# The order of the fill work in the middle stage of a two-layer diffusion block

## The chip, the cores and the metric

The kernel runs on one core of one Trainium2 chip, in fp32 (each matrix product as three matmuls on split operands, see below). The metric is the time of one execution on the device in microseconds, taken as the median of several runs.

## The reference

Two layers work on 256 tokens `x` and 256 context tokens `ctx`, each of width 1024. A layer is a SwiGLU feed-forward, a middle stage of three branches, and a second feed-forward; each has a norm with shift, scale and gate from a modulation vector. The change touches the middle stage only. Cut to that, for the tokens:

```python
zx = modulate(rms_norm(x, norm_g[l, 1]), mx[3], mx[4]) @ w_in[l]
qa, ka, va, qb, kb, vb, ux, gx = split_combined(zx)
qb, kb = apply_axial_rope(qb, cos, sin), apply_axial_rope(kb, cos, sin)
ya = neighborhood_attention(qa, ka, va, ka_c, va_c, na_rpb[l], rows)     # 6 heads
yb = window_attention(qb, kb, vb, kb_c, vb_c, sw_sink[l])                # 6 heads, 2 key heads
yc = conformer_conv(ux, conv_dw_w[l], conv_dw_b[l], conv_ln_g[l], conv_ln_b[l])
ga, gb, gc = jnp.split(jax.nn.sigmoid(gx + b_gate[l]), 3, axis=-1)
x = x + mx[5] * ((ga * (ya @ w_oa) + gb * (yb @ w_ob) + gc * (yc @ w_oc)) @ w_o)
```

`conformer_conv` is a gated linear unit, a depthwise convolution of 31 taps over 256 channels, a layer norm over the channels and a SiLU. The context tokens go through the same in layer 0; in the last layer (layer 1) only their keys and values are needed.

## The kernel before

All activations lie transposed, features on the 128 partitions and tokens along the free axis: 512 columns where both token sets are wanted (layer 0), 256 for `x` alone (layer 1). A product of fp32 accuracy is three matmuls (`mm3`, L316 to L320) on a high and a low part of both operands; the parts are made by `split` (L123): ACT copies the high part, DVE subtracts it for the low one. Weights stream in blocks of 512 KB; each half block is split the same way into `wh` and `wl`, a few blocks ahead of their use. One *step* of a product is one weight tile of 128 x 128, three matmuls.

The middle stage (`middle`, L679) first makes the keys and the gated input of the convolution, the values V and two queries. Then comes a loop (L1118 on) over the attention units `us`. A unit is a pair of heads and an index u: `kind` 0 is the neighbourhood branch, `kind` 1 the window branch, three pairs each; u runs over two halves of the queries of `x` and, in layer 0, a third unit for the context. In round n the program writes:

- `qk`: the scores of unit n into PSUM (`sc`, L987); for the window branch they need the rotated key `kb` and query `qb`;
- `turn`: for the unit before, when a pair's two halves are there, the transposes of the normalised weights `pf` (`pt`, L1048), copied and split by ACT and DVE;
- `soft`: the softmax of unit n on DVE and ACT (L1003 or L1009, exponentials L1020, scaling L1032);
- some steps of the *fill*;
- `pv`: the product with V for the unit before (L1067), and at a pair's end its output `y` (L1075, L1076 and a split).

The fill is a chain of generators (L1088) that is walked a step at a time: the third query of the neighbourhood branch (`query(2)`), gates (`gate(b, f)`, eight steps each, a tanh on ACT at L913; b is the branch, 0 neighbourhood, 1 window, 2 convolution; f one of eight blocks of 128 features), the window branch's key and queries (`key_b`, `query_b`, eight steps each, with a rotation `rope` at L874 that goes through ACT, DVE, POOL, ACT and DVE), and the merges (`merge(b, f)`, L916), that is the output projection of a branch (two steps for the convolution, three for the neighbourhood; `mo`), its product with the gate on DVE (L931) and the sum over branches `M` on POOL (L936). The window branch's merges follow after the loop. The fill is spread evenly: after round n, `nfill * (n + 1) // (N + LA)` of its 208 steps should be done. Steps are taken ahead of that when scores need a query or key that the fill hasn't made yet (the `while` in the loop). Merges of the neighbourhood branch are held back (`before_a`) until its three pairs are done.

Which gates come early is set by `EARLY` (7 in layer 0, 16 in layer 1), over an order of branches 2, 0, 1. So in layer 0 seven gates of the convolution branch come ahead of the window branch's key and queries, in layer 1 all eight of the convolution and all eight of the neighbourhood.

The convolution's taps run on DVE (L791), one for every second fill step. Behind the last tap three parts of its layer norm are put off by a counter of program points (`after`, L758, counted by `tick`, twice as far in the last layer): `mean` 10 points later (mean by a matmul, `cmean` L804, subtraction, squares on ACT, L808), `sums` 8 points after that (sums of squares, L339, square root on ACT, L343, reciprocal and diagonal on DVE, L353), and `rest` 8 points on (the rstd spread over partitions by a matmul, L358, then scale, bias on POOL and SiLU; `yc` is ready at L834, L835). If the first merge of the convolution branch finds no `yc`, it writes out all that is left at once:

```python
        if b == 2 and not ys:
            run(cv, 1 << 20)
            flush()
```

The order in which instructions are written is the order in which each engine takes them, but for a few places where the scheduler interleaves two groups.

Of the kernel before, what the change touches and what calls it, by code (L numbers as in the profile page):

```python
# [19 lines left out]
KD = 8  # L20
# [60 lines left out]
N_POOL = 2  # L81
CV_V = (1, 1)
CV_PACE = (2, 2)
EARLY = (7, 16)
N_FIRST = {0: 3, 1: 7, 2: 5}


# [1 line left out]
def dit_block_kernel(ctx, tc, xT, vec, ident_d, const, crow, gfin, rpb, ws, ada0, adaT, out):  # L89
# [17 lines left out]
    def S(dt=F32, name="s"):  # L107
        return slots.tile([P, 2 * NQ], dt, tag="s", name=nm(name))
# [11 lines left out]
    def f32(ap):  # L120
        return ap.bitcast(F32)
# [12 lines left out]
    for k in range(KD):  # L134
# [19 lines left out]
        out=cs[:, :, 0:2], in_=vt[:, V_C:V_C + 2 * KD].rearrange("p (k s) -> p k s", s=2), func=AF.Silu  # L154
# [524 lines left out]
    def middle(l, norm, nxt):  # L679
        last = l == DEPTH - 1  # L680
# [30 lines left out]
        for parts in fb[:3]:  # L711
            kh, kl = S2("ka")
            for t, sl, b in parts:
                nc.scalar.activation(out=kh[:, sl], in_=t, func=AF.Identity, bias=b)
                nc.vector.scalar_tensor_tensor(
                    out=kl[:, sl], in0=t, scalar=b, in1=f32(kh[:, sl]), op0=ALU.add, op1=ALU.subtract)
            ka.append((kh, kl))
        sg = S(name="sg")
        for s, (pg, pu) in enumerate(zip(fb[3][:nst], fb[4])):
            t, sl, b = pg  # L720
# [4 lines left out]
                out=sg[:, sl], in0=sg[:, sl], scalar1=1.0, scalar2=1.0, op0=ALU.mult, op1=ALU.add)  # L725
            t, sl, b = pu
            nc.vector.scalar_tensor_tensor(
                out=hp[:, 0, s, CPAD:CPAD + NX], in0=t, scalar=b, in1=sg[:, sl], op0=ALU.add, op1=ALU.mult)
# [8 lines left out]
        def now(gen):  # L737
# [12 lines left out]
            out=hp[:, 1, :nst, CPAD:CPAD + NX],  # L750
# [7 lines left out]
        def after(n, fn):  # L758
            due.append([n * (2 if last else 1), fn])
# [13 lines left out]
        def conv():  # L773
            accs = [S(name="cacc") for _ in range(2)]
            cw = small.tile([P, 2 * CONV_W], F32, tag="cw", name=nm("cw"), bufs=1)
            o = V_CW + l * 2 * CONV_W
            nc.vector.tensor_scalar(
                out=cw, in0=vt[:, o:o + 2 * CONV_W], scalar1=0.5, scalar2=None, op0=ALU.mult)
            def wide(t):
                return t[:, qs].rearrange("p (s t) -> p s t", t=NX)  # L780

            for j in range(CONV_W):
                for c in range(2):
                    acc, o = accs[c], c * CONV_W + j
                    x, w = hp[:, c, :nst, j:j + NX], cw[:, o:o + 1]
                    if j == 0:
                        ob = V_CB + l * 2 + c
                        nc.vector.tensor_scalar(
                            out=wide(acc), in0=x, scalar1=w, scalar2=vt[:, ob:ob + 1], op0=ALU.mult, op1=ALU.add)
                    else:  # L790
                        nc.vector.scalar_tensor_tensor(  # L791
                            out=wide(acc), in0=x, scalar=w, in1=wide(acc), op0=ALU.mult, op1=ALU.add)
                    yield
            taps = ring(N_TAP, F32, "ctap")
            sq, res = [], []
            gen = []

            def new(name):
                return next(taps)

            def mean():
                pm = PS("cmean")
                for c in range(2):
                    nc.tensor.matmul(pm[:, qs], onesC, accs[c][:, qs], start=c == 0, stop=c == 1)  # L804
                for c in range(2):
                    nc.vector.tensor_tensor(out=accs[c][:, qs], in0=accs[c][:, qs], in1=pm[:, qs], op=ALU.subtract)
                    q = new("csq")
                    nc.scalar.activation(out=q[:, qs], in_=accs[c][:, qs], func=AF.Square)  # L808
                    sq.append(q)
                after(8, sums)  # L810

            def sums():
                gen.append(inv_rms(sq, qs.stop, onesC[:, 0:1], res, new))
                next(gen[0])
                after(8, rest)

            def rest():
                next(gen[0], None)
                for c in range(2):
                    t = accs[c]  # L820
                    og, ob = V_LG + l * 2 + c, V_LB + l * 2 + c
                    nc.vector.scalar_tensor_tensor(
                        out=t[:, qs], in0=t[:, qs], scalar=vt[:, og:og + 1], in1=res[0][:, qs],
                        op0=ALU.mult, op1=ALU.mult,
                    )
                    nc.gpsimd.tensor_scalar(
                        out=t[:, qs], in0=t[:, qs], scalar1=1.0, scalar2=vt[:, ob:ob + 1], op0=ALU.mult, op1=ALU.add)

                    g = new("cg")
                    nc.scalar.activation(out=g[:, qs], in_=t[:, qs], func=AF.Tanh, scale=0.5)  # L830
                    nc.vector.scalar_tensor_tensor(
                        out=t[:, qs], in0=g[:, qs], scalar=1.0, in1=t[:, qs], op0=ALU.add, op1=ALU.mult)
                    h, lo = pair("yc")
                    nc.scalar.activation(out=h[:, qs], in_=t[:, qs], func=AF.Copy, scale=0.5)  # L834
                    nc.vector.scalar_tensor_tensor(  # L835
                        out=lo[:, qs], in0=t[:, qs], scalar=0.5, in1=f32(h[:, qs]), op0=ALU.mult, op1=ALU.subtract)
                    yc.append((h, lo))

            after(10, mean)

        cv = conv()
# [23 lines left out]
        def query(j):  # L865
            ps = yield from block(QA + j * P, qs)
            qh, ql = pair("q")
            nc.scalar.activation(out=qh[:, qs], in_=ps[:, qs], func=AF.Copy, scale=-QSCALE)
            nc.vector.scalar_tensor_tensor(
                out=ql[:, qs], in0=ps[:, qs], scalar=-QSCALE, in1=f32(qh[:, qs]),  # L870
                op0=ALU.mult, op1=ALU.subtract)
            qa.append((qh, ql))
# [13 lines left out]
        def key_b():  # L886
            ps = yield from block(KB, full)
            z = rope(ps, 1.0, full)
            kh, kl = S2("kb")
            split(kh[:, full], kl[:, full], z[:, full])  # L890
            kb.append((kh, kl))

        def query_b(j):
            ps = PS("qb")
            yield from steps(ps, [W.one("w_in_qb", l, k * P, j) for k in range(KD)], H, qs)
            z = rope(ps, -QSCALE, qs)
            qh, ql = pair("qx")
            split(qh[:, qs], ql[:, qs], z[:, qs])
            qb.append((qh, ql))
# [4 lines left out]
        def gate(b, f):  # L904
            pg = yield from block(GT + b * D + f * P, qs)
            if last and f % 2:
                g = gates[b, f - 1, 0][:, hc]
            else:
                gates[b, f, 0] = S(name="gate")
                g = gates[b, f, 0][:, qs]  # L910
            o = b * KD + f

            nc.scalar.activation(out=g, in_=pg[:, qs], func=AF.Tanh, bias=hb[:, o:o + 1], scale=0.5)  # L913
            gates[b, f] = g

        def merge(b, f):  # L916

            if (b, f) not in gates:
                yield from gate(b, f)
            g = gates.pop((b, f))  # L920
            ys = (ya, yb, yc)[b]
# [3 lines that stand above are left out]
            if b == 1:  # L925
                wts = [W.one("w_out_b_perm", l, j, f * P) for j in range(3)]
            else:
                wts = W.col("w_out_a" if b == 0 else "w_out_c", l, f * P, len(ys))
            ps = PS("mo")
            yield from steps(ps, wts, ys, qs)  # L930
            nc.vector.scalar_tensor_tensor(  # L931
                out=g, in0=g, scalar=1.0, in1=ps[:, qs], op0=ALU.add, op1=ALU.mult)
            if M[f] is None:
                M[f] = g
            elif b != 1:
                nc.gpsimd.tensor_tensor(out=M[f], in0=M[f], in1=g, op=ALU.add)  # L936
            else:
                nc.vector.tensor_tensor(out=g, in0=M[f], in1=g, op=ALU.add)
                h, lo = pair("m")
                split(h[:, qs], lo[:, qs], g)  # L940
                M[f] = (h, lo)
# [141 lines left out]
        def chain(*gens):  # L1083
            for g in gens:
                yield from g

        early = [(b, f) for b in (2, 0, 1) for f in range(KD)][:EARLY[l]]
        fill = chain(  # L1088
            query(2), *(gate(b, f) for b, f in early),
            key_b(), query_b(0), query_b(1), query_b(2),  # L1090
            *(merge(2, f) for f in range(KD)), *(merge(0, f) for f in range(KD)),
        )
        n_early = 5 * KD + len(early) * KD
        before_a = n_early + sum(2 + KD * ((2, f) not in early) for f in range(KD))
        nfill = before_a + sum(3 + KD * ((0, f) not in early) for f in range(KD))
        done = 0

        def step(n):
# [60 lines left out]
    for l in range(DEPTH):  # L1159
        last = l == DEPTH - 1  # L1160
# [137 lines left out]
```

## Time and profile before

| | us |
|---|---|
| median of 3 runs | 2006.89 (2006.39 to 2008.82) |
| the profiled execution, its own time | 2006.36 |
| its span, first to last instruction | 2004.6 |
| PE busy in the span | 1952.5 |
| middle stage's fill loop, layer 0 | about 484 to 705 |
| middle stage's fill loop, layer 1 | about 1618 to 1754 |

A row of the timeline gives the start from the span's beginning, the length and the instruction, output before `<-`, inputs behind it; `x16` is the number of instructions in the row, and a bracket is the idle time of the engine ahead of it with what ended it. Matmuls overlap, so what one costs is read from the start of one to the start of the next. Instructions with two passes (plain fp32 operands) count twice. Engine names: PE is TensorE, DVE VectorE, ACT ScalarE, POOL GpSimd.

### The profile page before, as it was taken

How to read it: one execution, taken by the hardware profiler on the slowest of the kernel's cores; microseconds unless marked ns; L12 is line 12 of the kernel's file. 1: busy time of each engine (PE TensorE's matmuls, PEld its weight loads, DVE VectorE, ACT ScalarE, POOL GpSimd, SP SyncE). 2: the span in 40 equal slices, each digit the busy share in tenths (PEclk: the TensorE clock that was granted, in tenths of full speed). 3: DMA queues.
4: the chain of work that ended last, by engine and by line, in shares of the span. 5: the costliest groups of instructions: out<-in, count | busy, mean ns of one | idle time of the engine just before them, and what ended most of it. 6: DMA issues, size and time to landing. Idle time of an engine off the chain costs nothing.

```text
span 2004.6 us, 29351 instructions
## 1 busy us (share of the span) xinstructions
PE 1952.5 (97%) x10722; PEld 1651.6 (82%) x10722; DVE 1411.7 (70%) x3188; ACT 914.7 (46%) x1763; POOL 105.3 (5%) x100
## 2 busy tenths in 40 slices
PE   7999999999969999999999999999999998899998
PEld 3788888897858888988888888888888988799998
DVE  5887777579656645876667659766674887877654
ACT  4533333354656744533333335333333567767553
POOL 0000000100010101100000010000001001200001
PEclk9999999999979999999999999999999999899999
DMA  7565555423212232354445524554453344255553
GB/s 289 169 202 187 162 175 179 139 90 106 73 41 68 86 99 90 109 177 160 149 157 166 180 90 165 169 156 159 158 168 121 104 140 137 69 184 181 189 185 111
DMA packets 82513, 287.40 MB, mean 143 GB/s; under 512 B 9152, under 2 KB 10944, under 8 KB 81984
## 3 DMA queue, kind: packets, MB, share of 16 engines
q1 hardware_dynamic: 79488, 277.91, 42.2%
q0 software_dynamic: 864, 4.98, 0.7%
q10 hardware_dynamic: 2016, 2.64, 0.4%
q8 instruction: 84, 1.38, 0.3%
q14 instruction: 61, 0.50, 0.1%
HBM read 284.44 MB, written 1.05 MB: 142 GB/s over the span
## 4 chain that ended last, share of the span: by engine, by line
PE 92%; DVE 3%; ACT 2%; DMA 1%; issue 1%; POOL 1%; ACTq 0%; DVEq 0%; POOLq 0%
PE g L319 13%; PE g L320 13%; PE g L318 13%; PE pr L319 8%; PE pr L320 8%; PE pr L318 8%; PE b L318 4%; PE b L319 4%; PE b L320 4%; PE f L318 3%; PE f L319 2%; PE f L320 2%; PE pt L1048 1%; PE sc L987 1%; PE pv L1067 1%; PE mo L318 1%
## 5 line engine op out<-in xcount | busy, mean ns | idle before, releaser
L124 ACT ACTIVATE wh<-raw 128x512 fp32r<-128x512 f32 x760 | 473.6, 631 | 749.4 <-PE g L319 266.4
L125 DVE TENSOR_TENSOR wl<-raw,wh 128x512 fp32r<-128x512 f32 x760 | 524.7, 696 | 187.8 <-PE pr L320 80.9
L245 DVE CUSTOM_DVE_ANT_0 junk<-araw,phase 128x512 f32<-128x512 f32 x512 | 354.8, 693 | 166.6 <-DMA araw<-in_adaT_dram 156.9
L319 PE MATMUL g<-Hl,wh 128*128 128x512 f32 (+1 forms) x1248 | 458.9, 368 | 1.7 <-DVE Hl L479 1.7
L320 PE MATMUL g<-Hh,wl 128*128 128x512 f32 (+1 forms) x1248 | 458.6, 368 | 0.0
L318 PE MATMUL g<-Hh,wh 128*128 128x512 f32 (+1 forms) x1248 | 456.8, 367 | 0.0
L319 PEld LDWEIGHTS g<-Hl,wh 128*128 128x128 f32 x1248 | 234.4, 188 | 44.6 <-DVE Hl L479 2.2
L318 PEld LDWEIGHTS g<-Hh,wh 128*128 128x128 f32 x1248 | 234.6, 188 | 42.7
L320 PEld LDWEIGHTS g<-Hh,wl 128*128 128x128 f32 x1248 | 234.7, 188 | 41.9
L318 PE MATMUL pr<-gh,wh 128*128 128x512 f32 (+1 forms) x704 | 257.6, 366 | 0.0
L320 PE MATMUL pr<-gh,wl 128*128 128x512 f32 (+1 forms) x704 | 257.4, 366 | 0.0
L319 PE MATMUL pr<-gl,wh 128*128 128x512 f32 (+1 forms) x704 | 257.2, 365 | 0.0
L318 PE MATMUL b<-Hh,wh 128*128 128x512 f32 (+1 forms) x480 | 164.8, 343 | 0.8 <-DVE pt L125 0.7
L320 PE MATMUL b<-Hh,wl 128*128 128x512 f32 (+1 forms) x480 | 162.9, 339 | 0.0
L319 PE MATMUL b<-Hl,wh 128*128 128x512 f32 (+1 forms) x480 | 162.8, 339 | 0.0
L319 PEld LDWEIGHTS pr<-gl,wh 128*128 128x128 f32 x704 | 132.2, 188 | 23.4
L318 PEld LDWEIGHTS pr<-gh,wh 128*128 128x128 f32 x704 | 132.3, 188 | 23.2
L320 PEld LDWEIGHTS pr<-gh,wl 128*128 128x128 f32 x704 | 132.2, 188 | 23.1
L318 PE MATMUL f<-qh,wh 128*128 128x258 f32 (+1 forms) x400 | 120.1, 300 | 0.4 <-ACT qh L505 0.4
L319 PE MATMUL f<-ql,wh 128*128 128x258 f32 (+1 forms) x400 | 115.8, 290 | 0.0
L320 PE MATMUL f<-qh,wl 128*128 128x258 f32 (+1 forms) x400 | 115.7, 289 | 0.0
L386 POOL TENSOR_TENSOR sq<-sq,sq 128x512 f32<-128x512 f32 (+1 forms) x36 | 44.1, 1226 | 1278.9 <-ACT sq L379 1276.9
(247 smaller groups left out, 2613.0 us busy)
## 6 DMA issues: line engine op xcount, KB each, us to landing
raw<-in_ws_dram SPq DMA_DIRECT2D x380, 512.0 KB, 3.5
araw<-in_adaT_dram SPq DMA_DIRECT2D x128, 512.0 KB, 4.1
araw<-in_ada_dram SPq DMA_DIRECT2D x32, 256.0 KB, 5.9
phase<-in_crow_dram POOLq DMA_DIRECT2D x3, 1024.0 KB, 6.7
tb<-in_rpb_dram ACTq DMA_DIRECT2D x12, 192.0 KB, 3.8
R<-in_xT_dram SPq DMA_DIRECT2D x8, 256.0 KB, 4.9
phase<-in_const_dram POOLq DMA_DIRECT2D x2, 640.0 KB, 6.3
out_dram<-fin SPq DMA_DIRECT2D x4, 256.0 KB, 2.5
```

Of the source, the lines that this page charges most:

```text
L124: nc.scalar.activation(out=hi, in_=src, func=AF.Copy)
L125: nc.vector.tensor_tensor(out=lo, in0=src, in1=f32(hi), op=ALU.subtract)
L245: nc.vector.tensor_tensor_reduce(out=junk, in0=raw[:, c], in1=self.rows[:, s, c], scale=1.0, scalar=0.0, op0=ALU.mult, op1=ALU.add, accum_ ...
L318: nc.tensor.matmul(ps, wh, xh, start=start, stop=False)
L319: nc.tensor.matmul(ps, wh, xl, start=False, stop=False)
L320: nc.tensor.matmul(ps, wl, xh, start=False, stop=stop)
L386: eng.tensor_tensor(out=a[:, full], in0=a[:, full], in1=sq[:, full], op=ALU.add)
L987: nc.tensor.matmul(pss[s][:, o], a[r, c], b[r, k], start=i == 0, stop=i == 2)
L1048: nc.tensor.transpose(pt[:, n * P:(n + 1) * P], self.pf[v][s][:, o + i * P:o + (i + 1) * P], ident)
L1067: nc.tensor.matmul(self.po[s][:, sl], V[t0 + i][j // 2][:, c:c + P], p[:, k], start=m == 0, stop=m == n - 1)
```

## The change

The chain of the fill is written in another order, and the norm's parts stand 14 points apart in place of 8. Neighbourhood merges now come ahead of convolution merges in both layers, so the early gates are those of the neighbourhood branch first. In layer 0 the seven early gates are replaced by those of branch 0, and the eighth of branch 0 and the first of branch 2 follow the queries. In layer 1 the sixteen early gates stay, but in groups between the key and queries of the window branch: six, key and first query, four, second query, three, third query, three. The number of fill steps stays 208; those ahead of the neighbourhood merges (`before_a`) go from 120 to 112 in layer 0 and from 184 to 168 in layer 1. One line less above it moves the code below by one line, and the new chain moves the last part by six.

```diff
-EARLY = (7, 16)
...
-                after(8, sums)
+                after(14, sums)
...
-                after(8, rest)
+                after(14, rest)
...
-        early = [(b, f) for b in (2, 0, 1) for f in range(KD)][:EARLY[l]]
-        fill = chain(
-            query(2), *(gate(b, f) for b, f in early),
-            key_b(), query_b(0), query_b(1), query_b(2),
-            *(merge(2, f) for f in range(KD)), *(merge(0, f) for f in range(KD)),
-        )
-        n_early = 5 * KD + len(early) * KD
-        before_a = n_early + sum(2 + KD * ((2, f) not in early) for f in range(KD))
-        nfill = before_a + sum(3 + KD * ((0, f) not in early) for f in range(KD))
+        ahead = {b: [(b, f) for f in range(KD)] for b in range(3)}
+
+        def some(b, n):
+            out, ahead[b][:n] = ahead[b][:n], []
+            return [gate(*bf) for bf in out]
+
+        if last:
+            parts = [query(2), *some(0, 6), key_b(), query_b(0), *some(0, 2), *some(2, 2), query_b(1),
+                     *some(2, 3), query_b(2), *some(2, 3)]
+        else:
+            parts = [query(2), *some(0, 7), key_b(), query_b(0), query_b(1), query_b(2), *some(0, 1), *some(2, 1)]
+        before_a = KD * len(parts)
+        nfill = before_a + sum((3 if b == 0 else 2) + KD * ((b, f) in ahead[b]) for b in (0, 2) for f in range(KD))
+        fill = chain(*parts, *(merge(b, f) for b in (0, 2) for f in range(KD)))
```

## The prediction

> **What bounds the kernel now.** The page first, its part on busy time: one engine is busy for nearly all of the span.
>
> ```profile
> PE 1952.5 (97%) x10722; PEld 1651.6 (82%) x10722; DVE 1411.7 (70%) x3188; ACT 914.7 (46%) x1763; POOL 105.3 (5%) x100
> ```
>
> The kernel is bound by TensorE, so the change can only win time in which PE idles or runs slowly. Second, PE's waits (what it waited for: us in total, times, longest).
>
> ```profile
> PE ada L201 <- DMA araw<-in_ada_dram: 12.6, 2, 11.8
> PE sc L987 <- ACT qx L124: 10.8, 3, 5.3
> PE sums L339 <- ACT ctap L808: 9.2, 1, 9.2
> PE mo L318 <- ACT ych L834: 4.8, 1, 4.8
> PE rstd L358 <- DVE ctap L353: 1.6, 1, 1.6
> ```
>
> The first is the kernel's start, which the change doesn't touch. The other four are all in the middle stages: the scores wait for the rotated query (qx), and the convolution's norm (sums, rstd) and its merge (mo) wait for each other. Third, the windows of the stretches in which they fall and of their neighbours (stretch, then its length, busy time of PE, PEld, DVE, ACT, POOL, the granted clock, DMA share, GB/s).
>
> ```profile
> 572.92:602.88 29.96, 14.40 (x59) 9.97 (x58) 14.50 (x29) 11.92 (x21) 5.13 (x6) 0.66 0.05 18
> 1612.37:1660.45 48.08, 47.31 (x384) 44.01 (x382) 40.58 (x106) 37.68 (x84) 0.00 (x0) 1.00 0.40 133
> 1660.45:1694.71 34.26, 34.26 (x261) 32.61 (x260) 21.93 (x44) 24.68 (x50) 3.75 (x4) 1.00 0.53 168
> 1694.71:1732.46 37.75, 26.96 (x142) 21.58 (x141) 31.35 (x77) 26.71 (x63) 5.23 (x6) 0.77 0.12 42
> 1732.46:1745.00 12.54, 12.54 (x107) 11.99 (x105) 11.74 (x33) 11.89 (x29) 2.91 (x3) 1.00 0.37 108
> ```
>
> The clock is part of the loss: 0.66 and 0.77 in the two stretches with waits, 1.00 in the others.
>
> **What goes in layer 0.** Before, PE reaches the first merge of the convolution branch (step 96 of the fill) when its norm has hardly begun, so `flush()` issues all of it on the spot:
>
> ```order
> L320 MATMUL qb_5139<-Hh_3722,wl_5035 128x512
> L804 MATMUL cmean_5190<-cacc_3986,onesC 128x512
> L339 MATMUL sums_5197<-onesC,ctap_5170 128x1
> L358 MATMUL rstd_5213<-ctap_5172,ones 128x512
> L318 MATMUL mo_5236<-ych_5220,wh_5040 128x512
> L1067 MATMUL pv_5243<-pt_4144,v_4117 128x256
> ```
>
> Now (lines one lower) gates (b), attention (pv, sc, pt) and the merges of the neighbourhood branch (mo from y) stand between:
>
> ```order
> L317 MATMUL qb_5139<-Hh_3722,wh_5034 128x512
> L317 MATMUL b_5190<-Hh_3639,wh_5040 128x512
> L803 MATMUL cmean_5267<-cacc_3986,onesC 128x512
> L1066 MATMUL pv_5207<-pt_4144,v_4121 128x256
> L986 MATMUL sc_5330<-kbh_4943,qxh_5029 128x512
> L338 MATMUL sums_5358<-onesC,ctap_5170 128x1
> L317 MATMUL mo_5383<-yh_4655,wh_5197 128x512
> L317 MATMUL mo_5383<-yh_5322,wh_5197 128x512
> L357 MATMUL rstd_5495<-ctap_5172,ones 128x512
> ```
>
> No matmul is added or taken away. What the old stretch cost is read from PE's timeline (start, length, what; a wait in brackets):
>
> ```profile
> 572.92 1.88 PE L804 MATMUL cmean<-cacc,onesC 128*128 128x512 f32 x4
> 583.99 3.67 PE L339 MATMUL sums<-onesC,ctap 128*128 128x1 f32 x16 [9.18 <-ACT ctap L808]
> 589.22 2.05 PE L358 MATMUL rstd<-ctap,ones 128*128 128x512 f32 x2 [1.57 <-DVE ctap L353]
> 596.08 0.80 PE L318 MATMUL mo<-ych,wh 128*128 128x512 f32 x1 [4.81 <-ACT ych L834]
> ...
> 599.11 2.10 PE L1067 MATMUL pv<-pt,v 128*128 128x256 f32 x16
> ...
> 602.88 0.48 PE L318 MATMUL mo<-ych,wh 128*128 128x512 f32 x1
> 603.20 0.39 PE L319 MATMUL mo<-ycl,wh 128*128 128x512 f32 x1
> 603.43 0.40 PE L320 MATMUL mo<-ych,wl 128*128 128x512 f32 x1
> ...
> 1679.68 0.95 PE L339 MATMUL sums<-onesC,ctap 128*128 128x1 f32 x8
> ```
>
> At full clock its content is: mean 1.88; sums 2 x 0.95 = 1.90 (layer 1 has half as many, at clock 1.00); rstd about 0.9 (2.05 at half clock); six merge matmuls at a spacing of 0.23 (603.20 to 603.43), 1.4; from pv to the next merge 602.88 - 599.11 = 3.77, left as it is. Sum 9.85 of 29.96: **20.1 us go**, 15.6 of them the three waits, the rest half-clock matmuls.
>
> What is late next there: between mean and sums now lie 33 matmuls of 0.23, a half pv (1.0) and scores (0.9), 9.5 us, against 9.2 that PE waited before; between sums and rstd, and rstd and the first convolution merge, over 11 us each, against 1.6 and 4.8. The third head pair's y is needed 6.3 us after its pv (scores 0.9, nine matmuls 2.1, sums 1.9, six merge matmuls 1.4). An earlier pair's y took 3.6 us, from copy to residue:
>
> ```profile
> 556.38 1.22 ACT L1075 ACTIVATE yf<-pv 64x512 f32<-64x512 f32 x2
> 559.33 0.69 DVE L125 TENSOR_TENSOR yl<-yf,yh 128x512 fp32r<-128x512 f32 x1
> ```
>
> The new wait lies between 0 and about 5 (the old wait for ych, were y as late); I take 0.5, since both covers exceed the rows that they have to hide.
>
> **What goes in layer 1.** Before, all sixteen gates came ahead of the key and the queries of the window branch. Its first scores need them, so at step 96 the program runs 56 fill steps in one lump, and the six window scores then have almost no fill between them:
>
> ```order
> L987 MATMUL sc_15118<-kbh_15038,qx_15101 128x512
> L1048 MATMUL pt_15126<-ident,pf_13949 128x128
> L1067 MATMUL pv_15168<-pt_13953,v_13926 128x256
> L987 MATMUL sc_15193<-kbh_15038,qx_15101 128x512
> L318 MATMUL qb_15246<-Hh_13452,wh_15049 128x256
> L987 MATMUL sc_15260<-kbh_15038,qx_15243 128x512
> ```
>
> Now a gate, a query and the mean stand between transposes and pv, and two gates behind the scores:
>
> ```order
> L986 MATMUL sc_14813<-kbh_14594,qx_14644 128x512
> L1047 MATMUL pt_14821<-ident,pf_13949 128x128
> L317 MATMUL b_14865<-Hh_13452,wh_14740 128x256
> L317 MATMUL qb_14901<-Hh_13452,wh_14780 128x256
> L803 MATMUL cmean_14933<-cacc_13795,onesC 128x256
> L1066 MATMUL pv_14943<-pt_13953,v_13926 128x256
> L986 MATMUL sc_14968<-kbh_14594,qx_14644 128x512
> L317 MATMUL b_15000<-Hh_13452,wh_14872 128x256
> ```
>
> The old stretch on PE, from the second query's end at 1694.71, and below it the same groups at full clock:
>
> ```profile
> 1700.21 0.79 PE L987 MATMUL sc<-kbh,qx 64*128 64x512 f32 x2 [5.34 <-ACT qx L124]
> ...
> 1701.79 3.57 PE L1048 MATMUL pt<-ident,pf 128*128 128x128 f32 x16
> ...
> 1714.50 0.50 PE L987 MATMUL sc<-kbh,qx 64*128 64x512 f32 x2 [1.93 <-ACT qx L124]
> ...
> 1715.41 3.59 PE L1048 MATMUL pt<-ident,pf 128*128 128x128 f32 x16
> ...
> 1727.59 0.80 PE L987 MATMUL sc<-kbh,qx 64*128 64x512 f32 x2 [3.52 <-ACT qx L124]
> ...
> 1732.46 0.36 PE L318 MATMUL mo<-yc,wh 128*128 128x256 f32 x1
> ```
>
> ```profile
> 1632.59 1.97 PE L1048 MATMUL pt<-ident,pf 128*128 128x128 f32 x16
> 1634.31 0.37 PE L318 MATMUL b<-Hh,wh 128*128 128x256 f32 x1
> ...
> 1734.67 2.04 PE L1067 MATMUL pv<-pt,v 128*128 128x256 f32 x16
> 1736.64 0.50 PE L987 MATMUL sc<-kbh,qx 64*128 64x512 f32 x2
> ...
> 1737.54 0.39 PE L318 MATMUL mo<-yc,wh 128*128 128x256 f32 x1
> 1737.77 0.28 PE L319 MATMUL mo<-yc,wh 128*128 128x256 f32 x1
> 1737.88 0.28 PE L320 MATMUL mo<-yc,wl 128*128 128x256 f32 x1
> ```
>
> Content: five scores of 0.90 (1736.64 to 1737.54), three times sixteen transposes of 1.72, two pv of 1.97, a query block of 24 matmuls at about 0.118 with 0.12 at its start, 2.95, and six merge matmuls, 0.83: 17.4 of 37.75. **20.4 us go**, 10.8 of them waits.
>
> What is late next: ACT and DVE. From 1660.45 to 1745.00 (three rows of the windows) PE needs 84.55 - 20.4 = 64.2 us; ACT was busy for 24.68 + 26.71 + 11.89 = 63.3 us in it, DVE for 65.0. The key's rotation moves ahead of that stretch, two steps on ACT like the one below and these on DVE:
>
> ```profile
> 1692.61 0.64 ACT L124 ACTIVATE kbh<-rot 128x512 fp32r<-128x512 f32 x1 [1.44 <-POOL rot L883]
> 1689.73 1.74 DVE L880 SCALAR_TENSOR_TENSOR rot<-b,phase 32x256 f32<-32x256 f32 x4 [0.17 <-ACT rot L877]
> 1693.39 0.88 DVE L125 TENSOR_TENSOR kbl<-rot,kbh 128x512 fp32r<-128x512 f32 x1
> ```
>
> That leaves ACT 63.3 - 1.2 = 62.1 and DVE 65.0 - 2.6 = 62.4, both 97% of PE's time. The row 1732.46:1745.00 has 95% and 94% with PE never waiting, so new waits can be 0. The longest stretch that ran well, 1612.37:1660.45, holds 78% of ACT and 84% of DVE; if 85% of ACT were the most that lasts, the same work would take 62.1 / 0.85 = 73.1 us, PE would wait 8.9, and three slow groups of transposes (3.57 against 1.97) would add 4.8: 13.7. I take 4.5, nearer to the first: the mix is the same, but the norm's table loads and the queries' rotations now stand in ACT's queue between the exponentials, which wait behind them, and the next transposes with these.
>
> Those loads are there before too, one row of them:
>
> ```profile
> 1680.47 1.28 ACT L343 ACT_TABLE_LOAD   x1
> 1681.77 0.26 ACT L343 ACTIVATE sd<-sums,eps 128x2 f32<-128x2 f32 x1
> ```
>
> They now lie between a pair's exponentials and its scaling, on which the next transposes wait. By this row the two switches hold ACT for 2.6 us, which the 63.3 contain. [...]
>
> **Edits at nothing.** Convolution taps keep their steps, weights the distance at which they are loaded (DMA share at most 0.53 above). POOL's adds move from the one branch to the other; in layer 1 eight follow within 16 steps, and the last branch's merges, eleven steps each, hide them; uncovered they'd cost the few us by which they trail.
>
> **The sum.** Against the profiled execution (2006.36, span 2004.6 and 1.8 around it; the median of the runs is 0.5 above): 20.1 + 20.4 - 0.5 - 4.5 = 35.5, so 1970.9; against the median, **1971.4**. No new wait at all gives 1966.4, both upper bounds, 5 and 13.7, give 1985.1; the forecast's own range is 1966 to 1977.
>
> **Rivals.** *ACT sets the pace* in layer 1: 13.7 in place of 4.5, 1980.6; for it the 97%, against it the row 1732.46:1745.00. Chance 0.18, for 1977 to 1982.
>
> *The rotated queries stay late.* The first scores came 8.4 us after their query's block (1694.71 - 2.95 to 1700.21). Now 72 matmuls of 0.118, a pv and a score lie between, 11.4 us; but the key's rotation precedes it on a busier ACT, which then stands waiting on POOL with the copies of y and the exponentials behind. All three late gives back 20.4 less the 4.5: 1987.3. Chance 0.08.
>
> *Slower: the clock stays down.* Place: layer 1's window loop, transposes behind scores. After a wait of only 1.93 the transposes at 1715.41 took 3.59, half clock. If a short gap in each round keeps PE there, 64.2 us of content take up to twice that; once two thirds of it do (40.5 saved of 60 lost) the kernel is slower, at worst 2026. Against it: 1.00 in 1612.37:1660.45, with 0.8 us idle. Chance 0.03. [...]
>
> *Nothing comes of it*: the lost time turns up elsewhere in the stage; the order above speaks against it. Chance 0.03, within 0.2% (about what a measurement of this kernel can tell from no change).
>
> **The numbers.** Forecast 0.68, rivals 0.18, 0.08, 0.03, 0.03. Faster 0.68 + 0.18 + 0.08 = 0.94, same 0.03, slower 0.03. The range goes from just under no new waits, 1965.5, to the end of the first rival, 1982.
>
> **What would show it.** Right: PE's waits for ctap, ych and qx gone or under 1 us each, clock 1.00 through layer 0's middle, the layer 1 window loop near 69 us from the same scores to the same transposes; what waits are left, transposes on pf or scores on qx. Wrong: waits of several us on pf, pt or y, or a clock below 0.9 in that loop.

## The result and the profile after

The changed kernel takes 1976.78 us (median of 4 runs, 1976.24 to 1977.84) against 2006.64 us before (2006.35 to 2008.82): a ratio of 0.985, 95% interval 0.9832 to 0.9867. That is 29.9 us less, where 35.5 were forecast; the time lies in the forecast's own range (1966 to 1977), 0.2 us inside its end. The first rival begins there, so the time alone doesn't tell the two apart. The profiled execution of the changed kernel took 1976.25 us, its span is 1974.5.

The page's line on busy time shows the same instructions in a shorter span: PE's busy time fell by 10.9 us, the rest of the 30.1 us between the spans was idle time.

```profile
PE 1941.6 (98%) x10722; PEld 1644.0 (83%) x10722; DVE 1406.1 (71%) x3188; ACT 909.7 (46%) x1763; POOL 103.5 (5%) x100
```

PE's waits after (us in total, times, longest). The rows for ctap and ych are gone, those for qx went from 10.8 to 0.7; small new ones stand in their place. Lines are one lower than before.

```profile
PE ada L200 <- DMA araw<-in_ada_dram: 13.3, 2, 12.2
PE pt L1047 <- ACT pf L1031: 3.6, 5, 1.1
PE b L317 <- DVE pt L124: 2.2, 2, 1.4
PE cmean L803 <- DVE rot L879: 1.7, 1, 1.7
...
PE sc L986 <- DVE qx L124: 0.4, 1, 0.4
...
PE sc L986 <- ACT qx L123: 0.3, 1, 0.3
```

Where the time came from is read by cutting both traces at the same instructions: the first V product of layer 0, the first of layer 1, and the first product with `w_o` (`pr`) of layer 1. The windows between them (stretch, length, busy time of PE, PEld, DVE, ACT, POOL, clock, DMA share, GB/s), first of before:

```profile
450.44:1590.06 1139.62, 1123.46 (x5406) 923.95 (x5404) 780.93 (x1758) 488.65 (x934) 55.96 (x47) 0.99 0.39 128
1590.06:1783.80 193.74, 182.19 (x1313) 167.01 (x1311) 159.78 (x368) 130.90 (x279) 18.78 (x20) 0.96 0.40 129
```

and of after:

```profile
451.85:1572.14 1120.29, 1117.77 (x5405) 921.28 (x5404) 779.55 (x1758) 486.49 (x934) 56.48 (x47) 1.00 0.40 130
1572.14:1752.77 180.63, 174.54 (x1312) 160.44 (x1311) 155.75 (x368) 128.24 (x279) 16.93 (x20) 1.00 0.42 138
```

Length less PE's busy time is PE's idle time. Layer 0 gained 19.3 us: idle time fell from 16.2 to 2.5 (13.6), busy time by 5.7, for the same matmuls. Layer 1 gained 13.1: idle time from 11.6 to 6.1 (5.5), busy time by 7.6. The start, up to the first V product, took 1.4 us longer (451.85 against 450.44), and what follows layer 1's `pr` 0.9 (1974.5 - 1752.77 = 221.7 against 2004.6 - 1783.80 = 220.8); the change touches neither, and in the twelve traces of the experiments the first V product starts anywhere from 451.1 to 453.0 and the last part takes 220.8 to 222.1, whatever the edit. The 450.44 of before lies 0.7 below that, so not all of the 1.4 is shown to be spread. 19.3 + 13.1 - 1.4 - 0.9 = 30.1.

In layer 0 the chain that PE had waited for now runs behind other work (PE's timeline of after: start, length, instruction, wait in brackets). Sums, root's spread and the merges of y come without a wait, at full clock (1.00 from 572 to 612); a wait that the prediction does not have stands ahead of the mean.

```profile
582.84 1.96 PE L803 MATMUL cmean<-cacc,onesC 128*128 128x512 f32 x4 [1.73 <-DVE rot L879]
...
594.33 1.84 PE L338 MATMUL sums<-onesC,ctap 128*128 128x1 f32 x16
...
596.81 0.39 PE L317 MATMUL mo<-yh,wh 128*128 128x512 f32 x1
...
607.26 1.02 PE L357 MATMUL rstd<-ctap,ones 128*128 128x512 f32 x2
```

The mean comes soon after the third window query's block, and `rot`, which the query's rotation writes, is no input of it; what it must wait for is a buffer that the rotation still reads, a PSUM bank by the code (an inference; the trace names only the rotation).

In layer 1 the largest new waits of the window loop stand at two groups of transposes, behind the first window scores. (Ahead of that loop two gate blocks wait 1.40 and 0.79 us for DVE's split of transposes, the 2.2 of the list above; before had one such wait of 0.7, and in the experiments the first of the two is anything from 0.3 to 1.9.)

```profile
1655.62 1.09 PE L1047 MATMUL pt<-ident,pf 128*128 128x128 f32 x8 [1.04 <-ACT pf L1031]
1657.78 0.99 PE L1047 MATMUL pt<-ident,pf 128*128 128x128 f32 x7 [1.06 <-ACT pf L1031]
```

ACT's timeline shows what made `pf` late: ACT stands for 2.10 us until POOL has finished the rotation of the first query, and a gate, weight copies and the softmax (exponentials L1019, scaling L1031) queue behind that copy.

```profile
1648.87 0.78 ACT L1074 ACTIVATE yf<-pv 64x256 f32<-64x256 f32 x2
1651.76 0.42 ACT L123 ACTIVATE qx<-rot 128x256 fp32r<-128x256 f32 x1 [2.10 <-POOL rot L882]
...
1653.49 0.69 ACT L1019 ACTIVATE pf<-sc,st 128x512 f32<-128x512 f32 x1
...
1654.85 0.72 ACT L1031 ACTIVATE pf<-pf,st 128x512 f32<-128x512 f32 x1
1655.47 0.67 ACT L1019 ACTIVATE pf<-sc,st 128x512 f32<-128x512 f32 x1
...
1657.01 0.71 ACT L1031 ACTIVATE pf<-pf,st 128x512 f32<-128x512 f32 x1
```

### The profile page after: what moved, and what is told of

Read it like the earlier page. It is cut to its first block, busy times and chain, and to the rows that moved or that the text cites. A ratio compares the mean times of both kernels' runs of the same rounds, so it can differ in the third digit from the quotient of the medians.

```text
span 1974.5 us, 29336 instructions
## 1 busy us (share of the span) xinstructions
PE 1941.6 (98%) x10722; PEld 1644.0 (83%) x10722; DVE 1406.1 (71%) x3188; ACT 909.7 (46%) x1763; POOL 103.5 (5%) x100
## 4 chain that ended last, share of the span: by engine, by line
PE 90%; DVE 4%; ACT 3%; DMA 2%; issue 1%; POOL 0%; ACTq 0%; SPq 0%; DVEq 0%; POOLq 0%
PE g L319 13%; PE g L318 13%; PE g L317 13%; PE pr L317 8%; PE pr L319 8%; PE pr L318 8%; PE b L317 3%; PE b L318 3%; PE b L319 3%; PE f L317 3%; PE f L318 2%; PE f L319 2%; PE mo L318 1%; PE mo L319 1%; PE mo L317 1%
```

## The experiments

Each edit is made on the changed kernel. The theory was the prediction's: two separate gains, one in each layer, the first from the norm's chain lying behind other work, the second from gates between the queries. Rivals were that one part does it all, that ACT's load is what is left in layer 1, and, once the trace was seen, that the rotation's place in ACT's queue is. Times are medians, in us. The runs went in three groups of four; a group shared a chip and the runs of before: 2006.85 in the first group, 2007.71 in the second, 2007.12 in the third. Only the third group has the changed kernel itself beside it; elsewhere "than the changed kernel" means the 1976.78 above, from another chip.

**Layer 0 alone** (layer 1 with the old list, convolution merges first).

```diff
-            parts = [query(2), *some(0, 6), key_b(), query_b(0), *some(0, 2), *some(2, 2), query_b(1),
-                     *some(2, 3), query_b(2), *some(2, 3)]
+            parts = [query(2), *some(2, 8), *some(0, 8), key_b(), query_b(0), query_b(1), query_b(2)]
...
+        order = (2, 0) if last else (0, 2)
...
-        fill = chain(*parts, *(merge(b, f) for b in (0, 2) for f in range(KD)))
+        fill = chain(*parts, *(merge(b, f) for b in order for f in range(KD)))
```

> Layer 0 in the new order, layer 1 with the old list of fill parts (all sixteen gates ahead of key and queries, convolution merges first); the norm parts stay 14 points apart. Theory A, the two layers' gains are separate: layer 1 gave 13.5 us in the profile of the changed kernel, so this run takes 1976.8 + 13.5 = 1990.3, and PE again waits about 10.8 us for qx. Rival, the stretches are coupled through the backlog of weights and buffers: under 1985 or over 1995.

Measured 1987.72 (ratio 0.9905, 0.989 to 0.9919), 19.1 less than before and 2.6 under theory A's number, outside the rival's ranges. PE waits again for qx, though 7.4 us and not 10.8. The later norm parts stay in layer 1 here, and in the old order the first convolution merge comes too early for them: a wait of 3.2 for `yc` is new. Layer 1's middle gains nothing by it, 193.6 us against 193.7 before.

```profile
PE sc L986 <- ACT qx L123: 7.4, 3, 4.0
PE mo L317 <- ACT yc L833: 3.2, 1, 3.2
```

**Layer 1 alone** (layer 0 with the old list).

```diff
-            parts = [query(2), *some(0, 7), key_b(), query_b(0), query_b(1), query_b(2), *some(0, 1), *some(2, 1)]
+            parts = [query(2), *some(2, 7), key_b(), query_b(0), query_b(1), query_b(2)]
...
+        order = (2, 0) if not last else (0, 2)
...
```

> Layer 1 in the new order, layer 0 with the old list (seven convolution gates first, convolution merges first, the norm written out at once). Theory A: the kernel before less 13.5 us, 2006.6 - 13.5 = 1993.1, with PE's waits for ctap and ych (15.6 us together) back in layer 0. Rival, coupling: more than 4 us off that.

Measured 1996.49 (0.9949, 0.9934 to 0.9964), 10.4 less and 3.4 short of theory A's number. In its trace layer 1's middle is 12.2 us shorter than before; the start, layer 0 and the end, which stand in the old order here, are 2.3 longer together, with nothing in them that the edit should change. Layer 0's three waits are back, as they were in before:

```profile
PE sums L338 <- ACT ctap L807: 9.2, 1, 9.2
PE mo L317 <- ACT ych L833: 4.8, 1, 4.8
...
PE rstd L357 <- DVE ctap L352: 1.6, 1, 1.6
```

19.1 + 10.4 = 29.5, against 29.9 for both: the gains are separate and add up within the few us that single parts differ by.

**The norm's parts as near as before.**

```diff
-                after(14, sums)
+                after(8, sums)
...
-                after(14, rest)
+                after(8, rest)
```

> The new order, but the norm's parts 8 points apart as before. Theory A, the order alone moves the norm away from the merge, and the distance of 14 only makes sure that its chain is done: in layer 0 eight points after the mean are some 5 to 6 us on PE, and the squares were ready about 7 us after the mean, so PE waits 1 to 3 us at sums: 1977.8 to 1980. Rival, the distance does most of layer 0's work: 1985 or more. Second rival, it does nothing: 1976.8 within 0.5.

Measured 1979.41 (0.9861, 0.9845 to 0.9878), 2.6 more than the changed kernel, with runs that overlap (1977.45 is the lowest here, 1977.84 the highest there). The size lies in theory A's range, the place was wrong: PE does not wait for the norm in layer 0. The new wait is in layer 1, in the middle of a gate, for a weight's low part:

```profile
1694.84 0.41 PE L319 MATMUL b<-Hh,wl 128*128 128x256 f32 x1 [2.70 <-DVE wl L124]
```

On DVE the norm's last part (cacc, yc) now falls among the rotation and the softmax ahead of that low part:

```profile
1687.14 1.28 DVE L879 SCALAR_TENSOR_TENSOR rot<-qb,phase 32x256 f32<-32x256 f32 x3
1688.65 0.88 DVE L830 SCALAR_TENSOR_TENSOR cacc<-ctap,cacc 128x256 f32<-128x256 f32 x2 [0.23 <-ACT ctap L829]
...
1690.36 0.76 DVE L834 SCALAR_TENSOR_TENSOR yc<-cacc,yc 128x256 fp32r<-128x256 f32 x2 [0.38 <-ACT yc L833]
...
1694.10 0.69 DVE L124 TENSOR_TENSOR wl<-raw,wh 128x512 fp32r<-128x512 f32 x1
```

Behind that wait the matmuls of 128x256 stand 0.21 us apart in place of 0.118, until 1698.5. So the distance of the norm's parts is worth at most 2 to 3 us of the 29.9, little more than the spread of runs; nearly all is the order of the fill.

**Layer 1's gates in one piece**, neighbourhood merges still first.

```diff
-            parts = [query(2), *some(0, 6), key_b(), query_b(0), *some(0, 2), *some(2, 2), query_b(1),
-                     *some(2, 3), query_b(2), *some(2, 3)]
+            parts = [query(2), *some(0, 8), *some(2, 8), key_b(), query_b(0), query_b(1), query_b(2)]
```

> The new order with one difference in layer 1: the sixteen gates come in one piece ahead of key and queries, as before; the neighbourhood merges stay ahead of the convolution merges. Theory A, layer 1's gain comes from gates that stand between the queries: all of the 13.5 us go, 1990.3, and PE waits about 10 us for qx. Rival, the order of the merges did it: 1976.8.

Measured 1988.23 (0.9906, 0.9891 to 0.9921), 11.5 more than the changed kernel. The waits for qx and the slow transposes behind them (sixteen took 3.67 us here, 3.57 and 3.59 in before, and 1.97 there where no such wait stood ahead) are those of before, so it is the gates between the queries that make the gain in layer 1, not the order of the merges.

```profile
1711.13 0.80 PE L986 MATMUL sc<-kbh,qx 64*128 64x512 f32 x2 [5.44 <-ACT qx L123]
...
1712.71 3.67 PE L1047 MATMUL pt<-ident,pf 128*128 128x128 f32 x16
```

**The query's split put off**, to try the rotation's place in ACT's queue.

```diff
...
-            split(qh[:, qs], ql[:, qs], z[:, qs])
+            later.append([6, lambda: split(qh[:, qs], ql[:, qs], z[:, qs])])
...
+                while h.kind and later:
+                    later.pop(0)[1]()
                 pss = h.qk(u)
```

> The changed kernel, but the high and low parts of a rotated window query are made up to six program points later (at the latest ahead of the window scores), so that ACT does not stand waiting for POOL's addition with a softmax queued behind it. Theory A (layer 1's new waits come from the rotation in ACT's queue): the two waits of transposes on pf behind the first window scores, about 1.05 us each, go; 2 us less than the changed kernel's 1976.8, 1974.8. Theory B (ACT's load as such sets the pace there): the copies only move, the same time is waited elsewhere, 1976.8 within 0.6.

Measured 1976.78 (0.9843, 0.9828 to 0.9857). This tells nothing: the first window scores are written right behind the rotation and need the split, so the copy kept its place, and its row on ACT reads as it did.

```profile
1651.59 0.42 ACT L123 ACTIVATE qx<-rot 128x256 fp32r<-128x256 f32 x1 [2.09 <-POOL rot L888]
```

**Two more table loads on ACT in layer 1**, the doubled cost.

```diff
...
+        if again:
+            ex = small.tile([P, 4], F32, tag="ex", name=nm("ex"), bufs=2)
+            nc.scalar.activation(out=ex[:, :nt], in_=sd[:, :nt], func=AF.Exp)
+            nc.scalar.activation(out=sd[:, :nt], in_=pt[:, :nt], func=AF.Sqrt, bias=eps)
...
```

> The changed kernel, and in layer 1 the convolution norm's root is taken twice with an exponential between the two (its result unused), so that ACT loads two tables more there, 2.6 us by the rows of before, and runs two small operations, about 0.5 us. Theory A (ACT has room in layer 1's loop): within 0.7 us of the changed kernel's 1976.8. Theory B (ACT sets the pace there, the first rival on record): about 3 us more, 1979.8, and more if transposes slow down.

Measured 1979.69 (0.9858, 0.9842 to 0.9875), 2.9 more: by the total, the ACT theory. The windows say otherwise. First the loop from layer 1's first scores to its last pv, then the merges behind it, of this kernel and below it of the changed one:

```profile
1601.04:1720.60 119.56, 113.33 (x888) 103.88 (x888) 98.99 (x250) 100.42 (x221) 10.78 (x14) 1.00 0.37 122
1720.60:1757.87 37.27, 35.18 (x283) 34.78 (x281) 29.82 (x55) 20.48 (x40) 5.33 (x6) 0.95 0.57 184
```

```profile
1600.20:1719.29 119.09, 113.08 (x887) 103.75 (x887) 100.86 (x255) 97.49 (x217) 11.62 (x15) 1.00 0.38 127
1719.29:1752.77 33.48, 33.40 (x282) 33.06 (x281) 27.23 (x51) 20.11 (x40) 4.84 (x5) 1.00 0.60 190
```

ACT works 2.9 us more inside the loop, and the loop is 0.5 longer, no more than executions of the changed kernel differ (119.95 in the second trace of it, see the last experiments): ACT has room there. The other 3.8 us come behind the loop, where ACT is busy for little more than half of the time. There DVE's program stands in another order (more weight splits and gate products ahead of the last pair's y), and PE waits 1.26 and 0.83 us for that y and then runs at half clock for some 3.4 us (128x256 at 0.21 and not 0.118, 1729.5 to 1732.7; granted clock 0.95 over the stretch). Why the edit moves DVE's order was not followed up, so the 2.9 in total stay in part unexplained.

**The mean of layer 0's norm four points later.**

```diff
-            after(10, mean)
+            after(10 if last else 14, mean)
```

> The changed kernel, with the mean of the convolution's norm in layer 0 four program points later (14 in place of 10), behind the third query's rotation. Theory A (the mean's wait of 1.73 us is for a PSUM buffer that DVE's rotation still reads): it goes and nothing is late in its place, 1.7 us less than 1976.8, 1975.1. Theory B: the wait moves to another matmul that needs that buffer, 1976.8 within 0.6.

Measured 1978.15 (0.985, 0.9835 to 0.9864): no gain. The wait for the rotation is gone, but without it PE reaches the neighbourhood merges 2.6 us earlier (594.22 against 596.81), the third pair's part before its y, and loses clock besides (128x512 at 0.43 to 0.47 and not 0.23):

```profile
594.22 0.40 PE L317 MATMUL mo<-yh,wh 128*128 128x512 f32 x1
...
596.08 0.50 PE L317 MATMUL mo<-yh,wh 128*128 128x512 f32 x1 [0.30 <-ACT yh L123]
597.58 0.51 PE L318 MATMUL mo<-yl,wh 128*128 128x512 f32 x1 [1.01 <-DVE yl L124]
...
599.86 0.67 PE L317 MATMUL mo<-yh,wh 128*128 128x512 f32 x1
600.33 0.63 PE L318 MATMUL mo<-yl,wh 128*128 128x512 f32 x1
600.76 0.63 PE L319 MATMUL mo<-yh,wl 128*128 128x512 f32 x1
...
603.32 0.44 PE L319 MATMUL mo<-yh,wl 128*128 128x512 f32 x1
603.59 0.39 PE L317 MATMUL mo<-yh,wh 128*128 128x512 f32 x1
```

**Both** the put-off split and the later mean:

> The later parts of the rotated queries and the later mean together, both as in the two runs named so. If both theories hold they add up: 1973.1. If neither does, 1976.8.

Measured 1978.30 (0.9853, 0.9839 to 0.9868), as the later mean alone.

**The first window query one gate earlier**, a second try at the rotation's place.

```diff
-            parts = [query(2), *some(0, 6), key_b(), query_b(0), *some(0, 2), *some(2, 2), query_b(1),
+            parts = [query(2), *some(0, 5), key_b(), query_b(0), *some(0, 3), *some(2, 2), query_b(1),
```

> The changed kernel with layer 1's key and first window query one gate (eight steps) earlier. On ACT the copies that begin the first query's rotation then stand ahead of a softmax and its parts behind it, so DVE and POOL work while ACT does. Theory A (layer 1's waits at the first window scores come from ACT standing 2.10 us for the rotation with the softmax behind): ACT's idle time there falls under 0.5 us, the two waits of transposes on pf of 1.04 and 1.06 us go, 2.1 us less than the changed kernel run beside it. Theory B (they come from ACT's and DVE's load): waits of the same sum turn up at these or the next transposes, within 0.7 us of it.

Measured 1974.23 (1973.13 to 1974.51; ratio to before 0.9839, 0.9826 to 0.9853), against 1977.08 (1975.32 to 1978.2) for the changed kernel run beside it: 2.9 less, and no run of the one overlaps one of the other. ACT now waits 0.85 us in place of 2.10, not under 0.5, and does so with the softmax ahead of it done:

```profile
1643.89 0.72 ACT L1031 ACTIVATE pf<-pf,st 128x512 f32<-128x512 f32 x1
1645.45 0.42 ACT L123 ACTIVATE qx<-rot 128x256 fp32r<-128x256 f32 x1 [0.85 <-POOL rot L882]
```

On PE the transposes behind the first window scores run without a wait:

```profile
1651.57 0.50 PE L986 MATMUL sc<-kbh,qx 64*128 64x512 f32 x2
...
1652.45 2.00 PE L1047 MATMUL pt<-ident,pf 128*128 128x128 f32 x16
```

So the two waits (1.01 and 1.06 in the trace run beside it) were the softmax behind the rotation, not ACT's load. The sum of the gain is another than expected: 1.0 us of new waits stand at the next window scores, for qx (0.71 and 0.28 more), and idle time in layer 1's middle falls by only 1.1. The other 1.8 of its 2.9 are busy time, most of it clock: in the trace run beside it the matmuls behind the two waits ran at half clock for some 3.5 us (1.6 lost, rows in the last section), and here they don't (clock 1.00 over layer 1's middle, 0.99 there).

**The third window query one gate earlier**, **both queries**, and **the changed kernel again**.

```diff
-                     *some(2, 3), query_b(2), *some(2, 3)]
+                     *some(2, 2), query_b(2), *some(2, 4)]
```

> The changed kernel with layer 1's third window query one gate earlier. Theory A (the waits of 0.34 and 0.45 us of the scores on qx are all that is left of the late queries): they go, 0.8 us less than the changed kernel run beside it. Theory B: the copies of y behind it come later and the time is the same within 0.5.

> Both, the first and the third window query each one gate earlier. If both theories A hold they add up, 2.9 us less than the changed kernel run beside it; if neither, the same within 0.7.

> The changed kernel itself, on the same chip as the three beside it, so that differences of one or two us can be read: 1976.8 within 1.5 by every theory.

Measured 1975.78 (1974.65 to 1977.42; 0.9849, 0.9835 to 0.9862), 1974.07 (1973.56 to 1974.48; 0.984, 0.9826 to 0.9853) and 1977.08 (0.9854, 0.984 to 0.9867). The third query's move alone is inconclusive: its runs overlap those of the changed kernel, and in its trace the scores' waits on qx go but a merge waits 1.5 us for a PSUM copy instead:

```profile
PE mo L317 <- DVE pt L124: 1.5, 1, 1.5
```

With both queries earlier the time is that of the first alone. The first alone and both are the best versions found, some 33 us under the kernel before.

## Why the prediction was right, and where the 5.4 us went

**The bound.** Right: PE's idle and half-clock time was all there was to win, and in both layers it went where the prediction said. Its signs came too: the waits for ctap and ych gone, 0.7 us for qx, clock 1.00 from 572 to 612, the window loop 66.9 us (1646.60 to 1713.55) where it said near 69. It is shorter than that because its content is: 61.5 us at the spacings of this trace, not 64.2, since the key's block of wide matmuls moved ahead of it too. Above its content it loses 5.5, not 4.5.

**Layer 0**, forecast 20.1 less 0.5: measured 19.3 (19.6 forecast). That the sum fits to 0.3 is luck: two errors stand against each other. The three waits are gone and so is the half clock (0.50 in the rows of sums and rstd before, 1.00 from 572 to 612 now). The 9.85 us of content were 1.2 too high: rows were taken at their full length where the next instruction starts earlier (in the changed kernel the mean costs 1.39 from start to start, the sums 1.70, rstd 0.46, against 1.88, 1.90 and 0.9), so busy time fell by 5.7 and not by 20.1 - 15.6 = 4.5. And the new wait was not the one bounded: y comes in time, and 1.73 us stand ahead of the mean, by the inference above for a buffer that the third query's rotation reads. Before, the mean stood right behind the query's block and waited for nothing; now half a gate's block, a pv, scores and transposes stand between, and it waits. With it and the smaller waits idle time fell by 13.6 where 15.6 - 0.5 = 15.1 were forecast. The later mean shows that wait and y are bound together: take the one away and the other is late.

**Layer 1**, forecast 20.4 less 4.5, that is 15.9: measured 13.1. The first term was right: at the spacings of the changed kernel's trace the old stretch's instructions take 17.3 us, where the working has 17.4. What was mis-sized is the 4.5 for new waits, in two ways. New waits are 5.3 (11.6 - 10.8 = 0.8 of the old idle time are other waits, and 6.1 are idle now), and 3.8 of them lie in the window loop that the working looked at, the rest at the gate blocks ahead of it. And PE loses some 1.7 us more than the rows of its waits say. A wait is counted from the end of the matmul before it, which takes 0.28 us, while without a wait the next would have started after 0.118; at eight waits this and its like come to 1.4. Together that is 7.0 in place of 4.5, nearly all of the 2.8 that are missing.

**What the new waits are** was put wrong in part. The prediction blamed ACT's load (97% of PE's time) with the norm's table loads and the queries' rotations in its queue. From the last neighbourhood scores to the wait ahead of the last transposes, ACT was busy for 88% of the time and DVE for 86%:

```profile
1646.60:1712.81 66.21, 62.40 (x498) 57.36 (x497) 57.01 (x145) 58.52 (x135) 7.12 (x10) 1.00 0.36 119
```

Two more loads made the loop only 0.5 longer. The rotations are the cause that was shown, for the two largest waits at pf: 2.1 us of them went with one query moved, while 1.0 came back at qx. The waits of the gate blocks for DVE's split of transposes were not tried.

**The rivals.** ACT as the pace of layer 1 falls by the two more loads, and its bound does too: 88% is above the 85% that it took as the most that lasts. The late queries fall: 0.7 us of waits for qx are left. The clock that stays down falls: it was 1.00 in the row above, with 3.8 us of waits in it. In the second trace of the changed kernel it did go down behind two of these waits, for some 3.5 us, and came back (last section). In one thing the second rival had the right mechanism at a small price: ACT standing for POOL (2.10 us) with exponentials behind it.

**The rest.** 1.4 us at the start and 0.9 after the middle stage lie where nothing was changed; single executions differ by as much, but for the part of the start said above. 0.3 + 2.8 + 1.4 + 0.9 is 5.4, the 35.5 forecast less the 30.1 of the spans.

## What to carry to other kernels

When a chain of small steps on other engines makes the bound engine wait, count what that engine has to do between the links, in its own instruction order: where the count exceeds the old wait, the wait can go, and the clock lost behind it too; here waits of 9.2, 4.8 and 1.6 us went, and the clock went from 0.66 (572.92 to 602.88 before) to 1.00 (572 to 612 now). Place a step that crosses three engines so that its last copy does not stand ahead of a softmax on the same engine; eight steps earlier were worth 2.9 us here (ACT stood for 0.85 us, not 2.10), while 2.9 us of added work on that engine made the loop only 0.5 longer. Judge the remaining waits by who is queued behind whom, not by the busy share.

## What was not expected of the hardware

In these traces the clock drops after some idle times of 1 to 2 us, and not after others. With the mean later PE idled for 0.30 and 1.01 us within 2.5 us, and 2.3 us after the second of these waits (597.58 to 599.86 above) the matmuls of 128x512 stood 0.43 to 0.47 us apart in place of 0.23. At 603.59, 3.7 us on, they were back. (Between the waits and the slow rows stand the sums, 1.7 us of matmuls of one column, and whether they have a part in it isn't shown.) Yet the wait of 1.73 us ahead of the mean cost no clock: 1.00 from 572 to 612, and no slow row behind it in any of the ten traces that have it.

The two waits for pf in layer 1 cost no clock in the trace of after (1.00 from 1655.62 to 1660.30), but here are the same waits in the second trace of the changed kernel:

```profile
1654.50 1.09 PE L1047 MATMUL pt<-ident,pf 128*128 128x128 f32 x8 [1.01 <-ACT pf L1031]
1656.65 1.59 PE L1047 MATMUL pt<-ident,pf 128*128 128x128 f32 x7 [1.06 <-ACT pf L1031]
...
1658.26 0.41 PE L318 MATMUL b<-Hl,wh 128*128 128x256 f32 x1
1658.47 0.41 PE L319 MATMUL b<-Hh,wl 128*128 128x256 f32 x1
...
1660.35 0.28 PE L319 MATMUL b<-Hh,wl 128*128 128x256 f32 x1
```

The seven transposes take 1.59 us in place of 0.99, and the gate's matmuls stand 0.21 apart in place of 0.118 until 1660.2: 1.6 us lost. Of the nine traces that have these two waits, four show this and five don't. So what a short wait costs is not settled by its length, and versions that differ by one or two us need several executions.
